# RMS norms of a hybrid decoder trunk: token sums on all partitions and the inverse root over the row

## Chip, cores, metric

The kernel runs on one NeuronCore of a Trainium2 chip. The metric is device time of one execution in microseconds (us). Engines are named as in the profile: PE (TensorE matmul), PEld (its weight loads), DVE (VectorE), ACT (ScalarE), POOL (GpSimd), SP (SyncE, which issues most DMAs).

## What is computed

A trunk of two layers over 1040 tokens (16 learned ones ahead of 1024) of 1024 features, in float32. There are five RMS norms over the features, and one more over groups of 256 features inside the Mamba-2 mixer:

```
def rmsnorm(x, w):
    y = x * lax.rsqrt(jnp.mean(x * x, axis=-1, keepdims=True) + 1e-5)
    return y * w
...
for layer in range(2):
    h = h + mixer[layer](rmsnorm(h, norm_mix[layer]))
    h = h + sq_relu_mlp(rmsnorm(h, norm_mlp[layer]), ...)
h = rmsnorm(h, norm_final)
# inside the mixer of layer 1, for each of 8 groups of 256 features
g = g * lax.rsqrt(jnp.mean(g * g, axis=-1, keepdims=True) + 1e-5)
```

The mixer of layer 0 is a linear recurrence beside a state-space model, that of layer 1 is Mamba-2 in chunks of 128 tokens ("SSD").

## The kernel before

**Layout.** The residual stream h lies in SBUF with features on the 128 partitions (eight slabs, index k) and tokens along the row. Tokens go in three tiles, `TT` = (0, 400), (400, 384), (784, 256), or without the 16 extra tokens `TL`, whose first tile is 384 wide. Weights and activations are split into a high and a low fp32r half, and each product is three matmuls (`mm3`, L182 to L184).

**A norm before.** It has two parts.
- `token_sums` (L246): the squares of the slabs are accumulated on ACT, POOL and DVE into one tile (`square`, L274; `sums` adds two accumulators at L287, and the last tile of the final norm hands over two). Then, for every 128 tokens, a matmul takes the 128 tokens of the accumulator as weights and a single column of ones as the moving operand (L253): the sums land with tokens on partitions, one column per 128 tokens. DVE scales them and adds epsilon (L258), and `rsqrt` (L187) takes the inverse root of this [128, 2 to 4] tile by an integer first guess (L193, L194) and three Newton steps of three operations each (L196 to L198).
- `token_bcast` (L266): for every 128 tokens a matmul with the root, repeated over 128 columns, as weights and the identity as the moving operand spreads it over all partitions (L270). The row then lies in PSUM and is read from there.

With fp32 operands each such product is two instructions in the trace.

**Who uses it.** 39 norms in all.
- `raw_stats` (L1019) for the first norm; the row is copied to SBUF by ACT (L1025), and the projections multiply by it when they leave PSUM.
- `factors` (L310) where the norm is applied late: `up_unit` copies the row to SBUF (L373) and multiplies at L375; `late2` (L1248) copies it for the last tile of the Mamba-2 mixer.
- `norm` and `apply` (L316, L290), for the first two tiles ahead of the Mamba-2 mixer: L296 multiplies, ACT and DVE or POOL split the result at L298 and L300.
- `final` (L324): the last norm, its multiplications at L338 (POOL, from a copy that ACT makes at L334) and L340 (DVE), and the output DMAs.
- `ssd_norm` (L1435): 8 groups by 3 tiles. L1457 multiplies, L1469 and L1470 split into yh and yl, and the output projection (`ssd_wout`, L1475) takes these as operands.

**Order of the work.** The two parts are steps of Python generators: between them other work is put out (`tick`, L133; `step`, L1542), in the SSD stretch some 18 us of PE work. The builder orders each engine's instructions by priority, which is the order in which they were written, moved by the offsets in `SHIFT` (L64) for `token_sums` and `token_bcast` among others. Each engine then runs its own list in order. PSUM has four buffers for product tiles (`mm`) and four small ones (`sm`), but two `mm` and three wide ones while the MLPs run. The sums and the row of a norm share one `sm` buffer.

**Other lines named below.** L176 and L177 split a weight tile (ACT cast, DVE or POOL difference). L1281, L1286 and L1287 take the SSD projections out of PSUM, through the short convolution and a tanh; L1302 and L1303 do so for the gates. L1390 and L1391 make the decay matrix of a chunk on ACT from a row that a DMA brings, POOL multiplies it (L1392), and L1406 uses it on PE. L1485 adds a projected tile to h. L599 and L607 add the MLP's result to h and scale it for the final norm. L922 and L923 are gate products of the layer 0 recurrence and their sigmoids, L927 an exponential, L1225 an exponential of the SSD time steps, L806 a transposition.

Of the kernel before, what the change touches and what calls it, by code (L numbers as in the profile page):

```python
# [18 lines left out]
P = 128  # L19
# [59 lines left out]
class Trunk:  # L79
    def __init__(self, ctx, tc, A, out, dbg=None):  # L80
        self.ctx, self.tc, self.nc, self.A, self.out = ctx, tc, tc.nc, A, out
        self.dbg = dbg or {}
        nc = self.nc
        self.cp = ctx.enter_context(tc.tile_pool(name="cp", bufs=1))
        self.wp = ctx.enter_context(tc.tile_pool(name="wp", bufs=2))
        self.tp = ctx.enter_context(tc.tile_pool(name="tp", bufs=2))
        self.sp = ctx.enter_context(tc.tile_pool(name="sp", reuse_waits="tile", bufs=2))
        self.pstack = None
        self.npsum = 0
        self.psum(False)  # L90
        ctx.callback(lambda: self.pstack.close())
        self.dr = ctx.enter_context(tc.tile_pool(name="dr", bufs=1, space=DRAM))
        cp = self.cp
        self.H = cp.tile([P, KT, NTOK], F32, name="h")
        self.h = [self.H[:, :, o:o + w] for o, w in TT]
        self.HI, self.LO = (cp.tile([P, KT, NTOK], F32R, name=q) for q in ("hi", "lo"))
        self.hi, self.lo = ([q[:, :, o:o + w] for o, w in TT] for q in (self.HI, self.LO))
        self.cols = cp.tile([P, NCOLS], F32, name="cols")
        nc.scalar.dma_start(self.cols, A["cols"])

        self.ident2 = cp.tile([P, 240], F32, name="ident")
        nc.gpsimd.memset(self.ident2[:, P:], 0.0)
        self.ident = self.ident2[:, :P]
        make_identity(nc, self.ident)
        self.ones = cp.tile([P, 1], F32, name="ones")
        nc.gpsimd.memset(self.ones, 1.0)

        nc.scalar.copy(self.cp.tile([P, 1], F32, name="first"), self.ones)

        pt = self.sm()  # L110
        for _ in range(5):
            nc.tensor.matmul(pt[:, :240], lhsT=self.ident, rhs=self.ident2, start=True, stop=True)
        self.later = deque()
        self.stage = "a"
        self.acc, self.rbs = {}, {}
# [68 lines left out]
        nc.tensor.matmul(pt, lhsT=wlo, rhs=xhi, start=False, stop=last)  # L184


    def rsqrt(self, s, n, tag="rs", m=P):  # L187

        nc, tp = self.nc, self.tp
        y = tp.tile([P, n], F32, name=tag + "y")  # L190
        t = tp.tile([P, n], F32, name=tag + "t")
        yi = y.bitcast(I32)
        nc.vector.tensor_scalar(out=yi[:m], in0=s[:m].bitcast(I32), scalar1=1, scalar2=None, op0=ALU.logical_shift_right)  # L193
        nc.vector.tensor_scalar(out=yi[:m], in0=yi[:m], scalar1=-1, scalar2=0x5F3759DF, op0=ALU.mult, op1=ALU.add)  # L194
        for _ in range(3):
            nc.vector.scalar_tensor_tensor(out=t[:m], in0=y[:m], scalar=-0.5, in1=y[:m], op0=ALU.mult, op1=ALU.mult)  # L196
            nc.vector.tensor_tensor(out=t[:m], in0=t[:m], in1=s[:m], op=ALU.mult)
            nc.vector.scalar_tensor_tensor(out=y[:m], in0=t[:m], scalar=1.5, in1=y[:m], op0=ALU.add, op1=ALU.mult)  # L198
        return y

    def exp_acc(self, out, x, shape, pool, tag):

        nc = self.nc
# [39 lines left out]
        v.scalar_tensor_tensor(out=out, in0=x, scalar=0.0, in1=e, op0=ALU.max, op1=ALU.add)  # L243

    @shifted
    def token_sums(self, accs, w, nfeat, st):  # L246

        nc, tp = self.nc, self.tp
        ch = [(o, min(P, w - o)) for o in range(0, w, P)]
        n = len(ch)  # L250
        for i, (o, l) in enumerate(ch):
            for j, a in enumerate(accs):
                nc.tensor.matmul(st[:l, 508 + i:509 + i], lhsT=a[:, o:o + l], rhs=self.ones, start=j == 0, stop=j == len(accs) - 1)  # L253
        s = tp.tile([P, 4], F32, name="ts_s")
        l = ch[-1][1]
        f = n if l == P else n - 1
        kw = dict(scalar1=1.0 / nfeat, scalar2=EPS, op0=ALU.mult, op1=ALU.add)
        nc.vector.tensor_scalar(out=s[:, :f], in0=st[:, 508:508 + f], **kw)  # L258
        if f < n:
            nc.vector.memset(s[:, f:n], 1.0)  # L260
            nc.vector.tensor_scalar(out=s[:l, f:n], in0=st[:l, 508 + f:508 + n], **kw)
        y = self.rsqrt(s[:, :n], n)
        return st, y, ch

    @shifted
    def token_bcast(self, sums, w):  # L266

        st, y, ch = sums
        for i, (o, l) in enumerate(ch):
            self.nc.tensor.matmul(st[:, o:o + l], lhsT=y[:l, i:i + 1].broadcast_to([l, P]), rhs=self.ident[:l, :l], start=True, stop=True)  # L270
        return st[:, :w]


    def square(self, i, k, off, w, pool=False, end=False):  # L274
# [7 lines left out]
            nc.scalar.activation(out=sq, in_=self.h[i][:, k, off:off + w], func=AF.Square)  # L282
            (nc.gpsimd if pool or k % 2 == 0 and not end else nc.vector).tensor_tensor(out=a, in0=a, in1=sq, op=ALU.add)

    def sums(self, i, w):
        a, b, *rest = [self.acc.pop((i, k)) for k in (0, 1, KT - 1) if (i, k) in self.acc]
        self.nc.vector.tensor_tensor(out=a, in0=a, in1=b, op=ALU.add)  # L287
        return self.token_sums([a] + rest, w, 1024, self.sm())

    def apply(self, wname, i, off, w, rb):  # L290

# [32 lines left out]
    def final(self, i):  # L324

        nc = self.nc
        o, w = TL[i]
        off = o - TT[i][0]
        st = self.sums(i, w)
        yield  # L330
        rb = self.token_bcast(st, w)
        if i < 2:
            rc = self.scr("s1", w)
            nc.scalar.copy(rc, rb)  # L334
        for k in range(KT):
            hs = self.h[i][:, k, off:off + w]
            if i < 2 and k % 2:
                nc.gpsimd.tensor_tensor(out=hs, in0=hs, in1=rc, op=ALU.mult)  # L338
            else:
                nc.vector.tensor_tensor(out=hs, in0=hs, in1=rb, op=ALU.mult)  # L340
            if k % 2:
                nc.sync.dma_start(self.out[k - 1:k + 1, :, o - META:o - META + w].rearrange("k p n -> p k n"),
                                  self.h[i][:, k - 1:k + 1, off:off + w])
# [674 lines left out]
    @shifted  # L1018
    def raw_stats(self, i):  # L1019

        o, w = TT[i]
        for k in range(KT):
            self.square(i, k, 0, w)
        st = self.sums(i, w)
        self.nc.scalar.copy(self.rb[:, o:o + w], self.token_bcast(st, w))  # L1025

    def split_y(self, i):

# [406 lines left out]
    def ssd_norm(self, pg, g, i):  # L1435

        nc = self.nc
        v = nc.vector
        o, w = TL[i]
        y = self.prod[g, "z", i]  # L1440
        m = o - TT[i][0]
        acc, sq = (self.prod[g, k, i][:, m:m + w] for k in ("x0", "x1"))
        nc.scalar.activation(out=acc, in_=y[:, 0], func=AF.Square)
        nc.scalar.activation(out=sq, in_=y[:, 1], func=AF.Square)
        nc.gpsimd.tensor_tensor(out=acc, in0=acc, in1=sq, op=ALU.add)
        yield
        yield
        sums = self.token_sums([acc], w, 256, self.sm())
        yield
        if i == 0:  # L1450
            self.flush()
            self.wo[g] = [self.load_w(self.A["ssd_out"][2 * g + j], pg, "o", lo_pool=(j == 1)) for j in range(2)]
        wo = self.wo[g]
        yield
        rb = self.token_bcast(sums, w)
        for j in range(2):
            v.scalar_tensor_tensor(out=y[:, j], in0=y[:, j], scalar=self.col("gnorm", 2 * g + j), in1=rb, op0=ALU.mult, op1=ALU.mult)  # L1457
        if g == 7 and i != 1:

            pool, q, wt = ((self.px, "xbc0", 400), None, (pg, "xbc1", 384))[i]  # L1460
            yh, yl = ([pool.tile([P, wt], F32R, name=q, bufs=6) for _ in range(2)] for _ in range(2))
            for j in range(2):
                nc.scalar.copy(yh[j][:, :w], y[:, j])
                v.tensor_tensor(out=yl[j][:, :w], in0=y[:, j], in1=yh[j][:, :w].bitcast(F32), op=ALU.subtract)
        else:
            self.flush(8)
            yh = pg.tile([P, 2, 384], F32R, name="yh", bufs=2)
            yl = pg.tile([P, 2, 384], F32R, name="yl", bufs=2)
            nc.scalar.copy(yh[:, :, :w], y)  # L1469
            v.tensor_tensor(out=yl[:, :, :w], in0=y, in1=yh[:, :, :w].bitcast(F32), op=ALU.subtract)  # L1470
            yh, yl = ([q[:, j] for j in range(2)] for q in (yh, yl))
        yield
        self.wq += [(g, wo, (yh, yl), i, n) for n in range(KT)]
# [132 lines left out]
    def run(self, stages="abcd"):  # L1606
        tc = self.tc
        if "a" not in stages:
            for i in range(3):
                self.load_h(i)  # L1610
        else:
            self.stage = "a"
            self.mixer0()
        if "a" in stages or "b" in stages:
            with tc.tile_pool(name="mlp0", reuse_waits="tile", bufs=2) as mp:
                self.pcw = 1040
# [109 lines left out]
```

## Time and profile before

| | us |
|---|---|
| median of 3 runs | 2750.51 (2750.38 to 2751.53) |
| profiled execution | 2749.45 |
| its span, first to last instruction | 2747.70 |
| PE busy | 2660.3 (97%) |
| DVE busy | 1954.4 (71%) |
| ACT busy | 1072.5 (39%) |
| POOL busy | 1017.0 (37%) |

The profile is of one execution. Busy time of PE is the union of matmuls whose ends are modelled, and matmuls overlap, so what an instruction takes of PE's queue is read from start to start. The stages in order: mixer of layer 0 to about 365 us, MLP 0 to about 1090, the SSD mixer to about 2050, MLP 1 and the final norm to the end.

### The profile page before, as it was taken

Reading aid. Unit: us, or ns where it says so; the run is one execution under the profiler, and the core shown is the slowest. Engines: PE = TensorE matmul, PEld = TensorE weight load, DVE = VectorE, ACT = ScalarE, POOL = GpSimd, SP = SyncE. Lnnn points to the kernel's source line nnn. Section 1 sums busy time; section 2 is a strip of 40 time slices with the busy share of each in tenths; the row PEclk is TensorE's granted clock in tenths of the full one; section 3 lists DMA queues with packets and bytes.
Section 4 is the critical chain, followed back from the end, with each engine's and each line's share of the span. In section 5 each row is a group of like instructions: output and inputs, shape, how many; then the busy total and the mean of one; then the engine's idle time right before and its main releaser. Section 6 shows DMA issues by size and latency. Waiting matters only on the chain.

```text
span 2747.7 us, 44368 instructions
## 1 busy us (share of the span) xinstructions
PE 2660.3 (97%) x17121; PEld 2545.9 (93%) x17121; DVE 1954.4 (71%) x3821; ACT 1072.5 (39%) x2162; POOL 1017.0 (37%) x826
## 2 busy tenths in 40 slices
PE   7888999999999999999999999999989999999998
PEld 7877999999999999899999999998988999999998
DVE  9977465666666686876867768677786666666685
ACT  5555343323332334443433434334454332333334
POOL 3101115444444432142332323323444554554542
PEclk9999999999999999999999999999999999999999
DMA  4432411111111110121221212213311111111111
GB/s 163 123 74 59 140 47 55 39 55 50 44 58 43 47 47 26 52 81 60 75 62 52 80 56 76 62 52 100 107 52 66 55 50 51 54 51 50 47 43 62
DMA packets 117907, 176.33 MB, mean 64 GB/s; under 512 B 13376, under 2 KB 47936, under 8 KB 117568
## 3 DMA queue, kind: packets, MB, share of 16 engines
q1 hardware_dynamic: 117408, 173.34, 20.2%
q8 instruction: 135, 2.21, 0.3%
q14 instruction: 76, 0.62, 0.1%
q10 hardware_dynamic: 288, 0.15, 0.0%
HBM read 158.34 MB, written 8.72 MB: 61 GB/s over the span
## 4 chain that ended last, share of the span: by engine, by line
PE 51%; DVE 6%; POOL 1%; ACT 1%; issue 1%; DMA 0%; SPq 0%; DVEq 0%; ACTq 0%; POOLq 0%
PE mm L182 12%; PE mm L183 12%; PE mm L184 12%; PE pd L182 3%; PE pd L184 3%; PE pd L183 3%; DVE xbc L1286 1%; PE sm L1410 1%; PE mm L1406 1%; PE mm L1403 1%; PE sm L1372 1%; PE sm L253 1%; PE sm L270 0%; DVE xbc L1288 0%; PE sm L1386 0%
## 5 line engine op out<-in xcount | busy, mean ns | idle before, releaser
L182 PE MATMUL mm<-hi,whi 128*128 128x384 f32 (+4 forms) x3120 | 1017.3, 326 | 10.4 <-ACT whi L176 8.6
L183 PE MATMUL mm<-lo,whi 128*128 128x384 f32 (+4 forms) x3120 | 1005.9, 322 | 0.9 <-DVE lo L300 0.5
L184 PE MATMUL mm<-hi,wlo 128*128 128x384 f32 (+4 forms) x3120 | 1003.0, 322 | 2.7 <-POOL wlo L177 2.7
L182 PEld LDWEIGHTS mm<-hi,whi 128*128 128x128 f32 x3120 | 589.7, 189 | 20.4 <-ACT whi L176 9.4
L183 PEld LDWEIGHTS mm<-lo,whi 128*128 128x128 f32 x3120 | 589.7, 189 | 7.2 <-DVE lo L300 0.8
L184 PEld LDWEIGHTS mm<-hi,wlo 128*128 128x128 f32 x3120 | 591.5, 190 | 3.7 <-POOL wlo L177 3.5
L182 PE MATMUL pd<-pc 128*128 128x260 f32 (+1 forms) x1176 | 377.1, 321 | 6.2 <-DVE s L375 2.2
L184 PE MATMUL pd<-pc 128*128 128x260 f32 (+1 forms) x1176 | 374.9, 319 | 0.0
L183 PE MATMUL pd<-pc 128*128 128x260 f32 (+1 forms) x1176 | 373.8, 318 | 0.0
L492 DVE TENSOR_TENSOR h<-h,pd 128x520 f32<-128x520 f32 (+1 forms) x336 | 291.9, 871 | 59.5 <-PE pd L184 45.2
L375 DVE SCALAR_TENSOR_TENSOR s<-mm,rb 128x384 f32<-128x384 f32 (+2 forms) x192 | 98.7, 515 | 266.6 <-PE mm L184 252.4
L389 POOL TENSOR_TENSOR pc<-ca,pc 128x512 fp32r<-128x512 f32 x112 | 169.4, 1513 | 244.9 <-ACT pc L388 164.3
L389 POOL TENSOR_TENSOR pc<-draw,pc 128x512 fp32r<-128x512 f32 x84 | 125.4, 1492 | 336.2 <-ACT pc L388 336.2
L182 PEld LDWEIGHTS pd<-pc 128*128 128x128 f32 x1176 | 221.7, 189 | 22.0 <-DVE acc L492 4.4
L184 PEld LDWEIGHTS pd<-pc 128*128 128x128 f32 x1176 | 221.8, 189 | 15.9
L183 PEld LDWEIGHTS pd<-pc 128*128 128x128 f32 x1176 | 221.9, 189 | 12.5
L176 ACT CAST whi<-wraw 128x512 fp32r<-128x512 f32 x286 | 167.8, 616 | 164.5 <-PE mm L183 144.0
L376 ACT ACTIVATE sq<-s 128x384 f32<-128x384 f32 (+2 forms) x192 | 94.1, 491 | 346.6 <-DVE s L375 346.5
L492 DVE TENSOR_TENSOR acc<-acc,pd 128x520 f32<-128x520 f32 (+1 forms) x234 | 190.4, 862 | 4.3 <-PE pd L184 4.1
L177 DVE TENSOR_TENSOR wlo<-wraw,whi 128x512 fp32r<-128x512 f32 x224 | 167.7, 767 | 19.9 <-ACT whi L176 11.5
L1392 POOL TENSOR_TENSOR csb<-csb,sc 128x512 f32<-128x512 f32 x64 | 89.7, 1401 | 211.2 <-DVE sc L1388 200.1
L388 ACT CAST pc<-cb 128x520 fp32r<-128x520 f32 (+1 forms) x112 | 70.0, 625 | 247.7 <-PE pd L184 130.8
(388 smaller groups left out, 4478.0 us busy)
## 6 DMA issues: line engine op xcount, KB each, us to landing
wraw<-in_mlp_up SPq DMA_DIRECT2D x128, 256.0 KB
wraw<-in_ssd_in SPq DMA_DIRECT2D x120, 256.0 KB
draw<-in_mlp_down SPq DMA_DIRECT2D x112, 256.0 KB
csb<-csd SPq DMA_DIRECT2D x64, 256.0 KB
ecb<-ecd SPq DMA_DIRECT2D x128, 64.0 KB
wraw<-in_ssd_out SPq DMA_DIRECT2D x32, 256.0 KB
wraw<-in_ev_in SPq DMA_DIRECT2D x24, 256.0 KB
wraw<-in_ev_out SPq DMA_DIRECT2D x18, 256.0 KB
```

Source lines behind the costliest of these rows:

```text
L176: nc.scalar.copy(h, raw)
L177: e.tensor_tensor(out=l, in0=raw, in1=h.bitcast(F32), op=ALU.subtract)
L182: nc.tensor.matmul(pt, lhsT=whi, rhs=xhi, start=first, stop=False)
L183: nc.tensor.matmul(pt, lhsT=whi, rhs=xlo, start=False, stop=False)
L184: nc.tensor.matmul(pt, lhsT=wlo, rhs=xhi, start=False, stop=last)
L253: nc.tensor.matmul(st[:l, 508 + i:509 + i], lhsT=a[:, o:o + l], rhs=self.ones, start=j == 0, stop=j == len(accs) - 1)
L375: nc.vector.scalar_tensor_tensor(out=r, in0=pt[:, :w], scalar=0.0, in1=rbs[i], op0=ALU.max, op1=ALU.mult)
L376: nc.scalar.activation(out=dst[:, o - t0:o - t0 + w].bitcast(F32), in_=r, func=AF.Square)
L388: nc.scalar.copy(hi, x)
L389: e.tensor_tensor(out=lo, in0=x, in1=hi.bitcast(F32), op=ALU.subtract)
L492: v.tensor_tensor(out=d, in0=d, in1=src, op=ALU.add)
L1392: nc.gpsimd.tensor_tensor(out=csb, in0=csb, in1=sc.unsqueeze(1).broadcast_to([P, 4, P]), op=ALU.mult)
```

## The change

All norms are computed in another form.
- `token_sums`: one matmul per accumulator with a full 128x128 matrix of ones as weights and the row of w accumulated squares as the moving operand. The sums land in PSUM already on all partitions. ACT then takes the logarithm (scaled by 1/n, with epsilon as bias, read from PSUM) and from it the exponential of minus one half of it: a first value of the inverse root, over the whole row, in SBUF.
- `token_bcast`: no matmul. Three DVE operations over the row make one Newton step, the second of them reading the sums in PSUM.
- `rsqrt` goes. The row now lies in SBUF: in `self.rb`, in a tile of a new pool `nr`, or in the accumulators of `ssd_norm`. The ACT copies in `raw_stats` and `final` go; those in `up_unit` and `late2` stay.

```diff
+        self.eps = cp.tile([P, 1], F32, name="eps")
+        nc.gpsimd.memset(self.eps, EPS)
...
-    def rsqrt(self, s, n, tag="rs", m=P):
...
     @shifted
-    def token_sums(self, accs, w, nfeat, st):
...
+    def token_sums(self, accs, w, nfeat, st, y):
+
+        nc = self.nc
+        for j, a in enumerate(accs):
+            nc.tensor.matmul(st[:, :w], lhsT=self.ones.broadcast_to([P, P]), rhs=a[:, :w], start=j == 0, stop=j == len(accs) - 1)
+        nc.scalar.activation(out=y, in_=st[:, :w], func=AF.Ln, scale=1.0 / nfeat, bias=self.eps)
+        nc.scalar.activation(out=y, in_=y, func=AF.Exp, scale=-0.5)
+        return st, y, nfeat
 
     @shifted
-    def token_bcast(self, sums, w):
...
+    def token_bcast(self, sums, w, t=None):
+
+        st, y, nfeat = sums
+        v = self.nc.vector
+        if t is None:
+            t = self.nr.tile([P, TW], F32, name="nrt")[:, :w]
+        v.scalar_tensor_tensor(out=t, in0=y, scalar=-0.5 / nfeat, in1=y, op0=ALU.mult, op1=ALU.mult)
+        v.scalar_tensor_tensor(out=t, in0=st[:, :w], scalar=nfeat * EPS, in1=t, op0=ALU.add, op1=ALU.mult)
+        v.scalar_tensor_tensor(out=y, in0=t, scalar=1.5, in1=y, op0=ALU.add, op1=ALU.mult)
+        return y
...
-    def sums(self, i, w):
+    def sums(self, i, w, y=None):
...
+        if y is None:
+            y = self.nr.tile([P, TT[i][1]], F32, name=f"nrm{i}")[:, :w]
+        return self.token_sums([a] + rest, w, 1024, self.sm(), y)
...
         rb = self.token_bcast(st, w)
-        if i < 2:
-            rc = self.scr("s1", w)
-            nc.scalar.copy(rc, rb)
...
-                nc.gpsimd.tensor_tensor(out=hs, in0=hs, in1=rc, op=ALU.mult)
+                nc.gpsimd.tensor_tensor(out=hs, in0=hs, in1=rb, op=ALU.mult)
...
-        st = self.sums(i, w)
-        self.nc.scalar.copy(self.rb[:, o:o + w], self.token_bcast(st, w))
+        self.token_bcast(self.sums(i, w, self.rb[:, o:o + w]), w, self.scr("s1", w))
...
-        sums = self.token_sums([acc], w, 256, self.sm())
+        sums = self.token_sums([acc], w, 256, self.sm(), sq)
...
-        rb = self.token_bcast(sums, w)
+        rb = self.token_bcast(sums, w, acc)
...
+        self.nr = self.ctx.enter_context(tc.tile_pool(name="nr", bufs=1))
```

## Rows read from the trace of the kernel before

**Rows 1.** The page: busy time of engines, and the chain that ended last.

```profile
PE 2660.3 (97%) x17121; PEld 2545.9 (93%) x17121; DVE 1954.4 (71%) x3821; ACT 1072.5 (39%) x2162; POOL 1017.0 (37%) x826
...
PE 51%; DVE 6%; POOL 1%; ACT 1%; issue 1%; DMA 0%; SPq 0%; DVEq 0%; ACTq 0%; POOLq 0%
```

**Rows 2.** Stretches: length, busy us of PE, PEld, DVE, ACT, POOL; clock, DMA.

```profile
1160.00:1860.00 700.00, 696.21 (x4670) 669.42 (x4669) 502.99 (x1226) 287.85 (x675) 224.23 (x213) 1.00 0.22 67
1860.00:2090.00 230.00, 212.16 (x1355) 199.33 (x1354) 183.86 (x434) 114.25 (x251) 100.56 (x90) 0.96 0.27 86
```

**Rows 3.** Whole span: busy PE and PEld of L253; L270's group by line.

```profile
0.00:2748.00 2748.00, 28.51 (x218) 30.55 (x218) 0.99 0.21 64
...
L270 PE MATMUL sm<-ident,rsy 128*128 128x128 f32 (+1 forms) x214 | 32.7, 283 | 11.1 <-DVE rsy L198 11.0
```

**Rows 4.** Timeline of PE, two places in the SSD stretch: start, length, instruction.

```profile
1349.85 0.72 PE L253 MATMUL sm<-ones,xbc 128*128 128x1 f32 x6
1350.43 0.37 PE L182 MATMUL mm<-hi,whi 128*128 128x260 f32 x1
...
1368.20 0.83 PE L270 MATMUL sm<-ident,rsy 128*128 128x128 f32 x6
1368.87 0.49 PE L1372 MATMUL sm<-ident,xbc 128*16 128x128 f32 x3
```

**Rows 5.** Timeline of PE, fp32 products of mixer 0.

```profile
106.83 2.69 PE L922 MATMUL mm<-h,gates 128*128 128x400 f32 x8 [0.76 <-DVE h L901]
109.35 0.27 PE L806 MATMUL sm<-ident,s5E 128*128 128x128 f32 x1
```

**Rows 6.** Waits of PE (us, times, longest); PE's timeline ahead of the SSD stretch.

```profile
PE sm L270 <- DVE rsy L198: 11.0, 9, 2.4
...
1094.21 0.93 PE L270 MATMUL sm<-ident,rsy 128*128 128x128 f32 x6 [1.05 <-DVE rsy L198]
1106.02 0.45 PE L182 MATMUL mm<-hi,whi 128*128 128x388 f32 x1 [0.57 <-ACT hi L298]
```

**Rows 7.** ACT: two groups by line and form; two places of its timeline.

```profile
L923 ACT ACTIVATE l_tr<-mm,cols 128x384 f32<-128x384 f32 x4 | 2.3, 577 | 0.7 <-PE mm L922 0.7
L282 ACT ACTIVATE s<-h 128x384 f32<-128x384 f32 x42 | 21.6, 518 | 25.8 <-DVE h L599 14.3 <-DVE rst L196 5.1 <-DVE h L1485 3.8
...
106.77 1.28 ACT L923 ACT_TABLE_LOAD   x1
108.06 1.43 ACT L923 ACTIVATE l_tr<-mm,cols 128x400 f32<-128x400 f32 x3
...
1147.41 1.28 ACT L1225 ACT_TABLE_LOAD   x1
1151.22 0.41 ACT L1225 ACTIVATE dec<-sm 128x288 f32<-128x288 f32 x1 [2.53 <-PE sm L1221]
```

**Rows 8.** ACT's longest wait, 1160 to 1860 us; timeline of ACT, then POOL.

```profile
ACT csb L1390 <- DMA csb<-csd: 127.1, 32, 8.2
...
1389.60 0.63 ACT L1391 ACTIVATE csb<-csb 128x512 f32<-128x512 f32 x1
...
1397.42 1.69 POOL L1392 TENSOR_TENSOR csb<-csb,sc 128x512 f32<-128x512 f32 x1 [9.56 <-DVE sc L1388]
```

**Rows 9.** DVE groups by line: a Newton line, and a row operation by form.

```profile
L197 DVE TENSOR_TENSOR rst<-rst,ts_s 128x3 f32<-128x3 f32 (+2 forms) x117 | 29.2, 250 | 2.0
...
L1288 DVE SCALAR_TENSOR_TENSOR xbc<-s,xbc 128x384 f32<-128x384 f32 x32 | 19.8, 619 | 0.3 <-ACT s L1287 0.3
```

**Rows 10.** Waits of PE for the split half yl (us, times, longest).

```profile
PE mm L183 <- DVE yl L1470: 1.6, 6, 0.4
```

**Rows 11.** The end of the kernel: timelines of ACT, PE and DVE.

```profile
2736.95 0.51 ACT L607 ACTIVATE h<-h,cols 128x256 f32<-128x256 f32 x1
...
2740.32 1.10 PE L270 MATMUL sm<-ident,rsy 128*128 128x128 f32 x4 [2.42 <-DVE rsy L198]
...
2741.46 2.74 DVE L340 TENSOR_TENSOR h<-h,sm 128x256 f32<-128x256 f32 x8 [1.19 <-PE sm L270]
```

More of the change, by code (lines that the diff above doesn't have):

```diff
@@ L184, in mm3 @@
         nc.tensor.matmul(pt, lhsT=wlo, rhs=xhi, start=False, stop=last)
-    def rsqrt(self, s, n, tag="rs", m=P):
[L189 to L199, printed above, removed]
     def exp_acc(self, out, x, shape, pool, tag):
@@ L245, in token_sums @@
     @shifted
-    def token_sums(self, accs, w, nfeat, st):
[L248 to L263, printed above, removed]
-    @shifted
-    def token_bcast(self, sums, w):
[L268 to L271, printed above, removed]
+    def token_sums(self, accs, w, nfeat, st, y):
[5 more added lines that the diff above has]
+        return st, y, nfeat
+    @shifted
+    def token_bcast(self, sums, w, t=None):
[7 more added lines that the diff above has]
+        return y
     def square(self, i, k, off, w, pool=False, end=False):
@@ L283, in square @@
             (nc.gpsimd if pool or k % 2 == 0 and not end else nc.vector).tensor_tensor(out=a, in0=a, in1=sq, op=ALU.add)
-    def sums(self, i, w):
+    def sums(self, i, w, y=None):
         a, b, *rest = [self.acc.pop((i, k)) for k in (0, 1, KT - 1) if (i, k) in self.acc]
         self.nc.vector.tensor_tensor(out=a, in0=a, in1=b, op=ALU.add)
-        return self.token_sums([a] + rest, w, 1024, self.sm())
+        if y is None:
+            y = self.nr.tile([P, TT[i][1]], F32, name=f"nrm{i}")[:, :w]
+        return self.token_sums([a] + rest, w, 1024, self.sm(), y)
     def apply(self, wname, i, off, w, rb):
```

## Prediction

> **What bounds the kernel now.** I began with the page: PE is busy for 97% of the span, and the chain that ended last lies on PE for just over half of it [rows 1]. The view by stretches shows how even this is: while the eight SSD groups run, PE is busy for 696 of 700 us at full granted clock, ACT for 288 and DVE for 503; only in the last group and the change of layers, 1860 to 2090 us, is PE free for 18 of 230 us [rows 2]. PE takes its work in order, so time taken off its queue shortens the run wherever nothing else is late; a stall costs in full.
>
> The norms' own share came next. The column sums (L253) are 218 instructions and the spreading of the root (L270) 214 [rows 3]. Their mean durations of 131 ns (28.51 by 218) and 283 ns aren't comparable prices, since matmuls overlap. The timeline gives what they hold of the queue: six sums from 1349.85 to the next matmul at 1350.43, 0.097 us each; six spreads from 1368.20 to 1368.87, 0.112 us each [rows 4].
>
> **PE's part of the change.** Removed: 218 x 0.097 = 21.1 us and 214 x 0.112 = 24.0 us, together 45.1. Added: one fp32 product per accumulator, 128 ones columns against w token columns. The nearest row is L922, also fp32 with 128x128 weights, two instructions per product: its first eight are, by the loop's order, products of 400, 384, 256 and 400 columns, and PE took 2.52 us from 106.83 to the next line's work at 109.35 [rows 5], so 1.75 ns per column. The widths in TT and TL give 3 x 1040 columns for the first three norms, 8 x 1024 for the SSD norms, 1024 for the second MLP's, and 1024 plus a second 256 for the final one (its last tile hands over two accumulators): 13,616 columns, 23.8 us. Net: **-21.3 us**, 16 x 0.58 + 8 x 0.38 = 12 us of it inside the SSD stretch (w = 384: 6 x 0.209 - 0.67; w = 256: 4 x 0.209 - 0.45). The uncertainty of the two issue prices is some 3 us.
>
> **PE's waits for the root.** PE now stands still nine times for the last Newton step, 11.0 us in all [rows 6]. L270 leaves PE, so these stops go; what is late next is the consumer. At 1094.21 a stop of 1.05 us goes, but the same norm's split pieces then stop PE at 1106.02 in any case [rows 6], and PE will arrive there earlier. One stop of 2.42 us belongs to the tail, counted below. Of the other 8.6 us I take half, **-4**; bounds 0 and -8.6.
>
> **ACT's part.** Ln isn't in this trace. Bounds for it: the PSUM-reading activation with a bias column, 577 ns at 384 columns, and the plain SBUF one, 518 ns, which I also take for Exp [rows 7]. A table load is 1.28 us [rows 7]. The trace has no Ln next to an Exp, so a norm may bring no load, one or two; I take two, since sigmoid and Exp, too, bring one each way. A norm then puts 0.58 + 0.52 + 2 x 1.28 = 3.66 us on ACT, 39 norms 143 us, against five PSUM copies that go. Where it hides: in the SSD stretch ACT waits 127 us in 32 gaps for the decay DMA alone, and the decay it makes is early: finished from 1389.60 on, picked up by POOL at 1397.42, after 9.56 us of waiting for DVE [rows 8]. The load needn't wait for PE: at 1147.41 one ran, then its Exp waited another 2.53 us for the matmul [rows 7]. So I cost the 24 SSD norms at nothing; without that cover it is up to 3.66 us each. Behind Ln in ACT's queue stand the evacuations of PSUM (L1281, L1302), the weight casts (L176) and the squares; DVE's weight halves and PE wait for those. At the layer changes and in the end stretch, where squares and casts stand close to PE's need, I take **+2** for 15 norms; bounds -3 and +12.
>
> The Trainium skill (page ScalarE: Activation LUTs, section What ACT_TABLE_LOAD costs) prices a switch at about 2.66 us, a drain of 1.38 us behind the load. Here the row disagrees: load at 106.77 for 1.28 us, next activation at 108.06 [rows 7]. By the page ACT would hold 78 x 1.38 = 108 us more and the tail grow by another 2.8 us, by the rows neither.
>
> **DVE's part.** Each norm loses twelve tiny operations; L197's three are 250 ns each, so twelve like them are 3.0 us per norm, 117 us in all [rows 9]. It gains three over the full row, like L1288's at 619 ns for 384 columns [rows 9]: 1.86 us per norm, some 63 us in all with the narrower tiles. DVE is relieved. But the place moves: the old work was done soon after the sums, the new three stand with the spreading, right ahead of the multiplication that needs them. In the SSD stretch some 18 us lie between sums and spreading (1349.85 to 1368.20 [rows 4]), so Ln and Exp are hidden there. For the first token tile of each group the way on is tight already: PE waited six times for the split half yl, 1.6 us [rows 10]. If all 1.86 us come before it, six stops cost 11 us; if the three run in DVE's gaps before, nothing. I take **+4**. Queued behind them on DVE are the conv steps L1286 and the residual adds L1485, which free PE's mm buffers; at 28% free time (197 of 700 us [rows 2]) these catch up. The final norm loses its ACT copies and POOL then reads the row directly; the multiplications keep their sizes: nothing.
>
> **The tail.** The last norm lies open. Now: spread at 2740.32, first multiplication at 2741.46; ACT's last square-side work ends at 2736.95 + 0.51 = 2737.46 [rows 11]. After: load to 2738.74, Ln 0.58, load 1.28, Exp 0.52, three row operations 1.86: 2742.98. That is **+1.5** (384-column prices for 256, so rather less); with no load at all -0.6; with the squares pushed back by the tile before, +3.
>
> **Sum.** -21.3 - 4 + 2 + 4 + 1.5 = -17.8 us. The profiled execution took 2749.45 us (span 2747.70 and 1.75 around it), 1.1 below the median of 2750.51; applied to the median this is 2732.7, rounded to 2732. About 0.2%, 5.5 us, is what a measurement of this kernel can tell from no change.
>
> **Rivals.**
> - *ACT's queue becomes the wait (slower).* Place: Ln stands in ACT's queue for the sums while a PSUM tile behind it isn't emptied, and PE runs out of its four mm buffers. Price: if half of 3.66 us reaches PE in the 24 SSD norms, 24 x 1.83 = 44 us against 25 gained: +19, **2769**. It decides from 25 / 39 = 0.65 us of PE stop per norm. For it: ACT is in order and the loads are new to this stretch. Against: rows 8. Chance 0.13.
> - *DVE's late row operations eat it.* All six tight places at 11 us, no stop recovered (0 for -4): -21.3 + 11 + 2 + 1.5 = -7, **2744**. For it: rows 10; against: DVE's gaps. Chance 0.14, half of it within 5.5 us of now.
> - *One load for Ln and Exp.* If both sit in one table, the load between them goes: the tail loses 1.28 us and each layer change as much in latency, some -3, **2729**. Only loads in front of other functions are in the trace. Chance 0.12. The Trainium skill (same page, Table sets: the hidden batching unit) says that one set holds both and that ln then exp costs one load; no run here shows it.
> - *Shorter chains.* Twelve hops on a crowded DVE become two on ACT and three on DVE; at the layer changes the root then comes early, all 8.6 us are kept and DVE's relief pays: -21.3 - 8.6 - 2 = -32, **2718**. Chance 0.09.
>
> My forecast has 0.52.
>
> **How the numbers follow.** Faster: 0.52 + 0.12 + 0.09 + 0.07 = 0.80; the same 0.07; slower 0.13. The range goes from 2714 (shorter chains, with 3 us of price error) to 2752 (the late row operations with +8 more at the layer changes); it leaves out the ACT rival and little else.
>
> **What would show it.** Right: L270 gone; L253 at 80 instructions, some 24 us of queue; PE's instructions down by 352; up to 78 more loads; no new PE wait on ACT in the SSD stretch. Wrong: PE waits for mm tiles whose release hangs on L1281 or L176, yl waits of over 1 us per group, or a first multiplication in the tail later than 6 us after the sums' start. The forecast is wrong if PE's busy time falls by 20 us and the span doesn't follow.

## The result, and the profile after

The changed kernel is slower: 2764.91 us median of 4 runs (2763.73 to 2766.59) beside 2750.45 us for the kernel before on the same chip (2747.55 to 2751.53, 4 runs). That is +14.5 us where -18 was forecast: outside the range, and on the other side. The ratio of the runs is given as 1.0065, 95% interval 1.0052 to 1.0077, a little above the quotient of these two medians (1.0053); by either it is slower. Here the two ways differ by 3 us, below by up to 2. The profiled execution has a span of 2762.0 us against 2747.7.

The busy times on the page of the kernel after, answering [rows 1]:

```profile
PE 2645.5 (96%) x16769; PEld 2523.2 (91%) x16769; DVE 1951.4 (71%) x3464; ACT 1207.0 (44%) x2312; POOL 1025.6 (37%) x827
```

The view by stretches, answering [rows 2, 3]: the SSD groups, and L238, the ones product, alone over the whole span (columns as there).

```profile
1176.00:1876.00 700.00, 692.94 (x4589) 664.57 (x4590) 502.86 (x1081) 355.83 (x755) 232.27 (x217) 1.00 0.23 68
...
0.00:2762.00 2762.00, 33.64 (x80) 15.01 (x80) 0.98 0.21 64
```

PE got its relief: 352 instructions fewer, 14.8 us less busy time, 80 instructions of ones products. In the SSD groups ACT is busy for 356 of 700 us instead of 288, and PE still for 693. The span did not follow. The waits of PE after, answering [rows 6, 10] (us, times, longest):

```profile
PE sm L238 <- DVE sa L269: 26.2, 9, 5.1
...
PE mm L185 <- DVE yl L1450: 0.2, 1, 0.2
```

The same stop before, ahead of the column sums, which the prediction didn't look at:

```profile
PE sm L253 <- DVE sa L287: 8.6, 6, 3.8
```

The stops for the root (L270) are gone, and so are those for yl; but PE now stands 26.2 us for the accumulator that the sums need. What is late there is DVE, and DVE waits for ACT. The waits of DVE at its first row operation (L250), by tile, and the table loads on ACT after, answering [rows 7]:

```profile
DVE xbc L250 <- ACT xbc L240: 34.9, 13, 3.0
...
DVE nrt L250 <- ACT nrm L240: 26.7, 11, 4.8
...
DVE s L250 <- ACT rb L240: 4.1, 2, 2.3
```

```profile
L239 ACT ACT_TABLE_LOAD x39 | 50.0, 1283 | 35.6 <-PE sm L238 35.1
L240 ACT ACT_TABLE_LOAD x37 | 47.5, 1283 | 0.7
```

All norms but two bring two loads of 1.28 us, 76 in all, and DVE stands 26 times, 65.7 us together, at the head of its queue for Exp. In the SSD groups (xbc, 34.9 us) nothing comes of it. At the layer changes (nrt) the residual additions (L580) and the square sums (L265, L269), which PE waits for, stand behind.

To see where the time went I followed five instants, one same instruction each, in the timeline of PE: the first of MLP 0's last products (before: 1042.49), the first SSD state product (1162.62), the first down product of MLP 1 (2079.34), the first of its last products (2686.78) and the end of the span (2747.7). After, they are at:

```profile
1048.75 0.45 PE L184 MATMUL mm<-acc,pc 128*128 128x400 f32 x1 [0.52 <-DVE s L356]
...
1176.51 0.66 PE L1390 MATMUL sm<-xte,btok 16*128 16x256 f32 x2 [1.02 <-DVE xte L1359]
...
2085.71 0.77 PE L184 MATMUL pd<-pc 128*128 128x512 f32 x1 [4.43 <-DVE s L356]
...
2693.50 0.44 PE L184 MATMUL mm<-acc,pc 128*128 128x384 f32 x1 [0.52 <-DVE s L356]
```

Five stages follow, by subtraction; the table gives before in us and each kernel's difference to it, for one profiled execution each (labels are those of the experiments below). A profiled execution is not the median one: that of e3 took 3.5 us more than its median, those of e9 and e12 3.3 and 3.2 less.

| kernel | mixer 0, MLP 0 | change to mixer 1 | SSD to MLP 1 | MLP 1 | tail | span |
|---|---|---|---|---|---|---|
| before | 1042.5 | 120.1 | 916.7 | 607.4 | 60.9 | 2747.7 |
| after | +6.3 | +7.6 | -7.5 | +0.4 | +7.6 | +14.3 |
| e1 new in SSD alone | +1.5 | +1.5 | -10.7 | +2.1 | 0.0 | -5.6 |
| e2 new outside SSD | +5.4 | +6.7 | +0.6 | +1.6 | +7.4 | +21.6 |
| e3 no loads | +3.7 | +3.4 | -17.8 | +0.6 | +0.7 | -9.4 |
| e8 loads behind | +3.2 | +7.1 | -7.1 | -1.0 | +2.2 | +4.4 |
| e9 root in PSUM | +7.9 | +0.8 | -8.2 | -1.0 | +3.5 | +3.0 |
| e10 no loads, PSUM | +1.8 | -3.9 | -17.6 | +0.5 | -3.3 | -22.5 |
| e11 mixed | +2.8 | -4.4 | -12.2 | +1.5 | -3.1 | -15.3 |
| e12 mixed, group 7 | -3.1 | -4.6 | -12.5 | +1.2 | -3.1 | -22.1 |

The first stage must be read with care: e11 and e12 have the same work there, and their two executions differ by 5.9 us. The kernels whose norms wait for loads there (after, e2, e9, and e7 with +12.0) have +5.4 to +12.0, the others but e5 -3.1 to +3.7, so a part of the +6.3 may be the loads; that is not shown. The other stages repeat within some 3.5 us where the code is the same (MLP 1 is the same in all).

The table leaves out PE's granted clock, which has two levels: 2.4 GHz (1.00 in the views) and 1.2 GHz (0.50). First the change to mixer 1 before, after and in e11; then six us of it after; then PE's ones product of 256 columns there, after and in e11 (columns as in [rows 2] and [rows 4]).

```profile
1042.49:1162.62 120.13, 113.82 (x710) 108.72 (x710) 91.92 (x226) 48.08 (x100) 24.85 (x24) 1.00 0.10 29
1048.75:1176.51 127.76, 115.03 (x678) 109.95 (x679) 94.33 (x199) 57.24 (x110) 25.05 (x24) 0.95 0.09 28
1045.32:1161.05 115.73, 110.06 (x679) 105.82 (x679) 92.86 (x202) 47.68 (x101) 24.23 (x24) 1.00 0.10 31
...
1116.00:1122.00 6.00, 4.96 (x15) 4.78 (x16) 4.20 (x10) 4.04 (x6) 0.71 (x1) 0.50 0.14 44
...
1117.05 1.22 PE L238 MATMUL sm<-sa,ones 128*128 128x256 f32 x2 [4.04 <-DVE sa L269]
...
1104.72 0.70 PE L240 MATMUL sm<-sa,ones 128*128 128x256 f32 x2 [2.09 <-DVE sa L278]
```

In the kernel after PE stood still for 4.04 us and then had 0.50 of the clock; the same product took 1.22 us instead of 0.70. For one instruction fewer than e11 PE is busy 5 us longer in this stage (115.03 and 110.06). So a stop cost more here than its own length. At the end of the SSD stage PE is busy for 86.19 us after at a clock of 0.92 and 81.89 in e10 at 0.96, in the tail for 50.81 at 0.87 and 47.96 at 0.94, with the same instructions.

The tail after, answering [rows 11]: timelines of DVE and PE, POOL's multiplications beside them, and ACT's last square-side work.

```profile
2738.47 0.56 DVE L250 SCALAR_TENSOR_TENSOR nrt<-nrm 128x384 f32<-128x384 f32 x1 [2.37 <-ACT nrm L240]
...
2741.06 5.11 DVE L321 TENSOR_TENSOR h<-h,nrm 128x384 f32<-128x384 f32 x4
2746.09 0.41 DVE L265 TENSOR_TENSOR sa<-sa,s 128x256 f32<-128x256 f32 x1
2746.43 0.74 DVE L580 TENSOR_TENSOR h<-h,mm 128x256 f32<-128x256 f32 x2
...
2749.56 0.42 DVE L269 TENSOR_TENSOR sa<-sa 128x256 f32<-128x256 f32 x1
...
2755.76 2.77 DVE L321 TENSOR_TENSOR h<-h,nrm 128x256 f32<-128x256 f32 x8
```

```profile
2750.03 1.22 PE L238 MATMUL sm<-sa,ones 128*128 128x256 f32 x2 [5.09 <-DVE sa L269]
```

```profile
2740.89 4.87 POOL L319 TENSOR_TENSOR h<-h,nrm 128x384 f32<-128x384 f32 x4 [8.76 <-DVE nrm L252]
...
2750.13 0.51 ACT L588 ACTIVATE h<-h,cols 128x256 f32<-128x256 f32 x1
```

Two things delay PE's last sums here. The row operations wait for Exp. Then four multiplications by the root hold DVE for 5.11 us while POOL does the other four; the residual additions of the last tile stand behind them. Before, the same four took 1.95 us:

```profile
2730.22 1.95 DVE L340 TENSOR_TENSOR h<-h,sm 128x384 f32<-128x384 f32 x4
```

### The profile page after: what moved, and what is told of

It is laid out like the page before. It is cut to its first block, busy times and chain, and to the rows that moved or that the text cites. A ratio compares the mean times of both kernels' runs of the same rounds, so it can differ in the third digit from the quotient of the medians.

```text
span 2762.0 us, 43481 instructions
## 1 busy us (share of the span) xinstructions
PE 2645.5 (96%) x16769; PEld 2523.2 (91%) x16769; DVE 1951.4 (71%) x3464; ACT 1207.0 (44%) x2312; POOL 1025.6 (37%) x827
## 4 chain that ended last, share of the span: by engine, by line
PE 76%; DVE 8%; ACT 3%; issue 2%; POOL 1%; DMA 0%; SPq 0%; ACTq 0%; DVEq 0%; POOLq 0%
PE mm L184 17%; PE mm L185 17%; PE mm L186 17%; PE pd L184 6%; PE pd L185 6%; PE pd L186 6%; PE sm L1390 1%; DVE xbc L1266 1%; PE mm L1386 1%; PE mm L1383 1%; PE sm L1352 1%; PE sm L238 1%; DVE wlo L179 1%; DVE xbc L1268 1%; ACT hi L291 0%
## 5 line engine op out<-in xcount | busy, mean ns | idle before, releaser
L184 PEld LDWEIGHTS mm<-hi,whi 128*128 128x128 f32 x3120 | 590.3, 189 | 30.5 <-ACT whi L178 11.3
L185 PEld LDWEIGHTS pd<-pc 128*128 128x128 f32 x1176 | 221.6, 188 | 12.2
```

The costliest lines, as they stand in the source:

```text
L184: nc.tensor.matmul(pt, lhsT=whi, rhs=xhi, start=first, stop=False)
L185: nc.tensor.matmul(pt, lhsT=whi, rhs=xlo, start=False, stop=False)
```

## Experiments

Theory A: the saving of the SSD groups arrives, and the loss sits at the start, the layer changes and the tail. Its causes as I came to see them: A1, the loads; P, the multiplications that now read the root from SBUF.

**e1, e2: one half each.**

```
# e1: kernel before, with the new functions under other names
-        sums = self.token_sums([acc], w, 256, self.sm())        # in ssd_norm alone
+        sums = self.row_sums([acc], w, 256, self.sm(), sq)
# e2: kernel after, the old functions in ssd_norm alone
```

> The new form in the 24 norms inside the SSD groups alone, the form of before in the 15 others. Theory A (the loss of 24 us sits at the start, the changes of layer and the tail; the saved PE work of the SSD groups arrives): the kernel is faster than before, by 9 to 13 us, near 2739 us; the two table loads per SSD norm cost PE nothing, and the PE waits at the layer changes are those of before (stops for the column sums near 9 us). Rival B (each of the 39 norms costs the kernel about the same, some 0.4 us): slower than before, near 2759. Rival C (the 10 us that the SSD groups seemed to gain were only time that PE had lost ahead of them, caught up): no gain, near 2750.

Measured: 2740.83 us beside 2747.09, ratio 0.9973 (0.9962 to 0.9985), some 7 us faster.

> The reverse: the new form in the 15 norms outside the SSD groups, the form of before inside them (its three small scratch tiles share one buffer for room). Theory A: the loss without the gain, near 2774 us (+24). Rival B: +6, near 2756. Rival C: the loss is the whole difference of the two kernels, +14, near 2765.

Measured: 2767.25 us, ratio 1.0066 (1.0053 to 1.0079), 18 us slower by the ratio, 20 by the medians. The signs are those of theory A, the sizes smaller (7 where 9 to 13 were expected, 18 to 20 where 24); B falls by both, C by e1. The table puts e2's loss where the changed kernel has it, and e1's gain in the SSD stage: from the first SSD product to the first product of 260 columns after 1900 us it took 800.9 us (1165.63 to 1966.49) against 815.5 before (1162.62 to 1978.07).

**e3: no loads.**

```
-        nc.scalar.activation(out=y, in_=st[:, :w], func=AF.Ln, scale=1.0 / nfeat, bias=self.eps)
+        nc.scalar.activation(out=y, in_=st[:, :w], func=AF.Identity, scale=1.0 / nfeat, bias=self.eps)
```

> The changed kernel with Ln replaced by Identity (same operands, scale and bias; the values of the roots are therefore not those of the reference). Every instruction of the change stays, but Identity is in the table that Exp uses, so 74 of the 76 table loads go. Theory A1 (the two loads, 2.56 us in each norm's chain, make DVE's first row operation and with it PE late): DVE's waits at that operation fall from 66 us to under 20, PE's stops at the ones product from 26 us to under 10, and the time falls to 2738 to 2746 us, below the kernel before. Rival A2 (two more steps on ACT's in-order queue and three full-row operations late on DVE do it, loads or not): 2758 to 2765.

Measured: 2736.54 us beside 2747.09, ratio 0.9955 (0.9942 to 0.9968). A1 holds: two loads are left, and the waits are

```profile
PE sm L238 <- DVE sa L269: 16.7, 7, 4.0
...
DVE nrt L250 <- ACT nrm L240: 8.9, 6, 3.1
DVE xbc L250 <- ACT xbc L240: 4.6, 6, 0.8
```

DVE's waits fall from 65.7 to 13.5 us as expected; PE's stops fall less than expected, 26.2 to 16.7 (under 10 was expected). By spans the loads cost 23.7 us (+14.3 against -9.4), by the ratios some 30; of the 23.7 they cost 6.9 in the tail, 10.2 from SSD to MLP 1, 4.2 at the change to mixer 1. Those 10.2 lie at the end of that stage: the steady groups took 803.6 us after (1176.51 to 1980.15) and 803.2 here (1169.73 to 1972.93), so in them the loads cost nothing. The stops are not all of it: after that product PE is busy for 82.00 us here, with one instruction fewer, and 86.19 after, at a granted clock of 0.96 and 0.92.

**e4: one activation and no load.**

```
-  Ln(scale 1/nfeat, bias eps); Exp(scale -0.5)
+  nc.scalar.activation(out=y, in_=st[:, :w].bitcast(I32), func=AF.Exp,
+                       scale=-0.5 * math.log(2) / 2 ** 23, bias=self.seed[nfeat])
+  # four row operations: t = 64/9/n*y*y; t *= st + n*EPS; t = (t - 10/3)*t; y = (t + 5)*y
```

> The changed kernel with one ACT instruction per norm instead of two: Exp alone, on the sum's bits read as an integer (an integer is 2^23 times a rough logarithm), and a cubic correction of four row operations on DVE in place of the Newton step of three. It computes the reference. Theory A1: as without the loads, less one ACT step and plus one row operation of 0.56 us per norm, 2738 to 2746 us. Rival A2: one ACT instruction less but one DVE operation more per norm, so still 2755 to 2765.

Measured: 2743.49 us beside 2747.09, ratio 0.9984 (0.9976 to 0.9993): inside A1's numbers, so the loads and not the change as such. From SSD to MLP 1 it gained 9.6 us, e3 17.8; the fourth row operation may be what takes the rest, but no run tried it alone.

**e5, e8: the loads, but nobody waits for them.** In e5 a Ln and an Exp on a constant column stand behind each norm's Exp.

> The kernel without loads (Identity in Ln's place, so other values for the roots) with a Ln and an Exp on one column added behind each norm's Exp: ACT does the two table loads again, 2.56 us and two tiny activations per norm, but nothing waits for their results. Theory A1a (the loads cost because DVE's first row operation waits for Exp behind them): the time stays near that without loads, 2737 to 2744 us, and DVE's waits at that operation stay under 25 us. Rival A1b (the loads cost because they hold up the squares and casts behind them in ACT's queue): most of the 25 us between the changed kernel and the one without loads comes back, 2755 to 2765, with PE's stops at the ones product over 22 us.

Measured: 2829.32 us beside 2746.68, and the test missed its aim. The added operations depend on nothing, so the order that the builder plans put them at the start: from 60.35 us on ACT does one load after another, and the first stage took 96 us more. The later stages are those of e3 within 2 us (123.4, 897.0, 606.4, 61.7 us). e8 ties them to the norm:

```
         nc.scalar.activation(out=y, in_=y, func=AF.Exp, scale=-0.5)
+        nc.scalar.copy(self.dum[:, :1], y[:, :1])
+        nc.scalar.activation(out=self.dum[:, 1:2], in_=self.dum[:, :1], func=AF.Ln, bias=self.ones)
+        nc.scalar.activation(out=self.dum[:, :1], in_=self.dum[:, 1:2], func=AF.Exp)
```

> The kernel without loads (Identity in Ln's place, so other values for the roots), with three operations on one column added on ACT behind each norm's Exp and tied to its result: a copy, a Ln and an Exp. So both table loads (2.56 us) and some 0.6 us of tiny activations stand on ACT per norm again, in their place, but nothing outside ACT waits for them. The earlier try let them run at the start. Theory A1a (the loads cost because the root, and with it DVE's first row operation, comes later): 2737 to 2745 us; DVE's waits at that operation under 25 us; the tail as without loads, within 2 us of 61.6. Rival A1b (they cost because they hold up what stands behind them on ACT): 2755 to 2765, PE's stops at the ones product over 22 us, as in the changed kernel.

Measured: 2753.81 us beside 2748.01, ratio 1.0023 (1.0014 to 1.0032), between the two theories, and the waits show both:

```profile
PE sm L239 <- DVE sa L273: 25.4, 7, 5.4
...
DVE sa L269 <- ACT s L268: 14.5, 17, 1.8
DVE nrt L254 <- ACT nrm L241: 9.0, 7, 3.1
```

DVE no longer waits for the root (9.0 us), but for squares that stand behind the loads on ACT (14.5 us; 8.5 in e3, 8.1 in the kernel after), and PE's stops are back at 25.4. Of the loads' 23.7 us, 13.8 are back (+4.4 against -9.4). Of these, 3.4 stand in the steady groups (806.6 us against 803.2 in e3), where the loads of the kernel after cost nothing; they can be due to the three small operations, so through ACT's queue it is some 10 us. The stages say where: the change to mixer 1 is as in the kernel after (127.2 and 127.8 us), and from the product of 260 columns to MLP 1 7.2 of 9.8 us are back (103.0 here, 95.8 in e3, 105.6 after), so there the queue decides; the tail has only 1.5 of its 6.9 us back, so there it is the chain.

**e6: without the last group.** `... if g < 7 else` the form of before.

> The new form in the 21 norms of SSD groups 0 to 6 alone; group 7, whose norms stand among the squares of the next layer, and all others in the form of before. With the new form in all eight groups the stretch from the last group to MLP 1 was 3.9 us longer than before. Theory A (the new form costs wherever its chain isn't covered, the last group included): those 3.9 us come back at the price of one eighth of the saving, so 1 to 4 us faster than with all eight groups, 2737 to 2740, and 2747 minus 9 or so. Rival (the 3.9 us belong to how the eight groups end earlier, waiting for weights): nothing comes back, 2741 to 2743.

Measured: 2739.32 us beside 2746.68, ratio 0.9971 (0.9962 to 0.9981). The time lies in theory A's range, but the ratio is that of e1 (0.9973), and from the product of 260 columns to MLP 1 it took 104.8 us, e1 105.2 and the kernel before 101.3. Nothing came back, so the last group's norms were not what that stage lost: it is 3.5 us longer than before with the same code.

**e7: row operations one turn later.** `yield; yield` in place of one `yield` in the three norms outside SSD.

> The changed kernel with the three row operations (and what follows them) of the norms at the layer changes and at the end issued one turn later, behind one more residual unit, Ln and Exp with both loads where they were. Theory A1a (DVE stands at the head of its queue for Exp while residual additions and square sums that PE needs stand behind): DVE's waits at the first row operation fall by a third or more, the stretch from the end of MLP 0 to the first SSD product falls from 127.8 us to 121 to 125, and the time to 2752 to 2760. Rival (the chain's own length decides: the normalized pieces come late, wherever DVE stands): no gain or a loss, 2763 to 2772.

Measured: 2767.48 us, ratio 1.0074 (1.0056 to 1.0091). It tells little: the planned order moved, but DVE's waits at L250 at the layer changes stayed (27.9 us for nrt), so the edit did not remove what it was to remove; the change to mixer 1 was 1.8 us shorter, the first stage 5.7 longer, which its scatter can give.

**e9, e10: the root back in PSUM**, in the kernel after and in e3.

```
-        v.scalar_tensor_tensor(out=y, in0=t, scalar=1.5, in1=y, op0=ALU.add, op1=ALU.mult)
+        y0, y = y, st[:, :w] if psum else y
+        v.scalar_tensor_tensor(out=y, in0=t, scalar=1.5, in1=y0, op0=ALU.add, op1=ALU.mult)
# psum=True in norm and final; in final, as before the change, for i < 2:
+            nc.scalar.copy(rc, rb)                # and POOL multiplies by rc
```

> The changed kernel with one thing as before: for the second mixer's first two norms and the final norm the last row operation writes the root back to PSUM, DVE's multiplications read it there, and POOL reads a copy in SBUF that ACT makes. In the changed kernel DVE's eight final multiplications of 384 columns took 1322 ns each with the root in SBUF while POOL multiplied too; before they took 550 ns with the root in PSUM. Theory P (two SBUF inputs on DVE collide with POOL's reads, and these 2 x 4 multiplications hold the residual additions behind them): the eight go back to 550 to 600 ns, the tail falls from 68.5 us to 62 to 65, the change of layer by 1 to 2 us, the time to 2756 to 2761. Rival Q (they are slow because they start late, or cost nothing that the end waits for): the tail stays over 67 us, the time 2763 to 2766.

Measured: 2755.95 us beside 2748.01, ratio 1.0027 (1.0016 to 1.0037): theory P, though the change to mixer 1 gained more than the 1 to 2 us expected. The groups of DVE by form, first the kernel after, then e9:

```profile
L321 DVE TENSOR_TENSOR h<-h,nrm 128x384 f32<-128x384 f32 x8 | 10.1, 1322 | 0.0
...
L280 DVE SCALAR_TENSOR_TENSOR s<-h,cols,nrm 128x400 f32<-128x400 f32 x8 | 6.1, 803 | 0.9 <-POOL lo L284 0.9
...
L321 DVE TENSOR_TENSOR h<-h,nrm 128x256 f32<-128x256 f32 x8 | 2.8, 419 | 0.0
```

```profile
L281 DVE SCALAR_TENSOR_TENSOR s<-h,cols,sm 128x400 f32<-128x400 f32 x8 | 4.7, 627 | 0.6 <-POOL lo L285 0.6
...
L325 DVE TENSOR_TENSOR h<-h,sm 128x384 f32<-128x384 f32 x8 | 3.9, 550 | 0.3 <-ACT s L319 0.2
```

With the root in PSUM the eight take 550 ns again, beside the same work on POOL; the last tile's eight (256 columns), which have no POOL work beside them, took 419 ns with the root in SBUF all the same. So it is the place of the operand together with POOL. By spans it cost 11.3 us (+14.3 against +3.0), by the ratios some 10: 6.9 at the change to mixer 1, 4.1 in the tail. Inside the SSD groups the root lies in SBUF, too, and there the multiplications of 384 columns (L1437) took 644 ns against 607 before.

> Both taken away: no loads (Identity in Ln's place, so other values for the roots) and the root in PSUM for these norms. If loads and port are the two separate causes, the gains add: without loads was 10.6 us under the kernel before, the port gives 4 to 8 more, so 2728 to 2733 us beside 2747, near the saving that was forecast. If the port matters only while the chain is late from the loads, 2735 to 2738.

Measured: 2726.74 us beside 2748.01, ratio 0.9918 (0.9906 to 0.9930), 21 us faster, just below the range. The two causes add: 23.7 and 11.3 us alone, 36.8 together (+14.3 against -22.5); by the ratios 30, 10 and 40. Some 10 of the 36.8 us are longer busy time of PE for the same 16769 instructions, 2645.5 us after and 2635.9 here, at a granted clock of 0.983 and 0.988 over the span.

**e11, e12: versions that beat both kernels.** e11 takes Ln, Exp and one Newton step inside SSD, e4's form elsewhere, and the root in PSUM; e12 gives e4's form to group 7 too.

> A version that should beat both kernels and computes the reference: inside the SSD groups the change as it is (Ln, Exp, one Newton step), where its loads are covered; outside, Exp on the sum's bits and the cubic step, so no load there, and the root in PSUM as above. Theory: the SSD saving of 10 us, the start and MLP 0 about as before, the changes of layer and the tail 0 to 3 us better than before: 2733 to 2738 us. If the late row operations on DVE cost by themselves at the layer changes: 2739 to 2743, no better than the new form in the SSD groups alone.

Measured: 2733.91 us beside 2748.01, ratio 0.9946 (0.9934 to 0.9959), 14 us faster than before and 31 faster than the change.

> The mixed version with the last SSD group's three norms also by Exp on the sum's bits and the cubic step, so that no norm outside groups 0 to 6 brings a table load. In the changed kernel the stretch from the last group to MLP 1 lost 9.8 us against the version without loads, while the steady groups lost nothing. If that loss is the loads of group 7's norms, which stand among the squares of the next layer: the stretch from the first SSD product to MLP 1 falls from 904.5 us to 898 to 901 and the time by 3 to 6 us, to 2728 to 2731 beside a before of 2748. If it is the later norms' loads (those of MLP 1, gone already in the mixed version) or the cubic step's extra row operation takes it back: within 2 us of the mixed version, 2732 to 2736.

Measured: 2730.57 us beside 2749.53, ratio 0.9937 (0.9924 to 0.9951). The total is in the first theory's reach, but its reason fails: the stretch from SSD to MLP 1 is 904.2 us against 904.5, and what e12's profile has over e11's lies in the first stage, where the two do the same work. So taking group 7's loads away gained nothing in this form; whether they cost nothing, or the fourth row operation takes back what they cost, this run doesn't tell. Of the 10 us at the end of that stage, MLP 1's own norms account for about 5: from that product of 260 columns to MLP 1 it took 105.6 us after, 100.7 in e11. Why e3 needs only 95.8 there stays open in part: its chain is one row operation shorter, and that alone was not tried. 1.8 of the 4.9 us between the two are PE's busy time, 83.81 us in e11 at a granted clock of 0.93 and 82.00 in e3 at 0.96, with the same instructions.

## Why the prediction was wrong

**PE's part was right.** Instructions fell by 352. The 12 us inside the SSD stretch came: 815.5 us before, 803.6 after, 803.2 without loads. PE's busy time fell by 14.8 us, not 20, and by 24.4 in e10 (2635.9 us) with the same instructions: the price of PE's work holds, and some 10 us of it went to the lower clock in the stages with stops. The prediction's "a stall costs in full" was too little: it cost more.

**PE's waits for the root (-4) and DVE's late row operations (+4)** cancelled in the sum and neither came as put. L270's stops went, and yl's waits went from 1.6 to 0.2 us instead of growing. The stops moved to the sums: 8.6 to 26.2 us. Nor was DVE relieved by 117 less 63 us: its busy time went from 1954.4 to 1951.4.

**The step that failed first is ACT's part**, "I take +2 for 15 norms; bounds -3 and +12". I priced what two loads do to ACT's queue, and let nothing wait for the root at the head of DVE's. The loads cost 23.7 us by spans, twice the upper bound: e8 shows some 10 through the squares and casts behind them on ACT; the rest, by e8's waits and tail, goes through the root that comes later. The prediction's own sentence on it (squares and casts "stand close to PE's need") named the place and underpriced it. For the norms of the steady SSD groups, "at nothing" was right; for the last group it is not told apart.

The reason given, "the load needn't wait for PE", holds in some norms only. Rows of ACT after, in one SSD group: in the first norm the load ran ahead and Ln waited, in the second the load itself began after the sums. The last row is from the view of line L239: six times the line has a semaphore instruction on ACT's queue, and their first and last start, 1284.7 and 1848.4, are those of the six loads that came late.

```profile
1359.92 1.28 ACT L239 ACT_TABLE_LOAD   x1
1362.90 0.58 ACT L239 ACTIVATE xbc<-sm,eps 128x384 f32<-128x384 f32 x1 [1.70 <-PE sm L238]
...
1397.51 1.28 ACT L239 ACT_TABLE_LOAD   x1 [5.84 <-PE sm L238]
...
L239 ACTq EVENT_SEMAPHORE  x6: 17/17/17, 1284.7 to 1848.4; - x6
```

**The second is half a sentence**: "the multiplications keep their sizes: nothing". They keep their sizes and not their durations, 550 to 1322 ns, since the root moved from PSUM to SBUF. That was 11.3 us by spans, more than any term of the sum but PE's, and it could have been asked of [rows 11], which names the PSUM operand. The Trainium skill (page SBUF — State Buffer, section Who interferes with whom) states that a DVE instruction with two SBUF inputs contends with a GpSimd instruction that reads SBUF; these rows agree.

**The tail** was put at +1.5 and took +7.6: without loads +0.7, with the root in PSUM as well -3.3. What the term priced came nearly as put: from the end of ACT's last square-side work to the first multiplication it is 5.1 us after (2750.64 to 2755.76) and 4.0 before (2737.46 to 2741.46), +1.1. The other 6.5 us came before the last sums, where the tile ahead held DVE; the term took their start as unchanged and kept +3 for squares pushed back.

**The rivals.** The one on the slower side gave 2769, close to the 2764.9 measured, and is no more right than the forecast: its place was the SSD stretch and PE's buffers, and there nothing was lost. One load for the pair did not come (39 and 37 loads); the Trainium skill's sentence for it (page ScalarE: Activation LUTs, section Table sets: the hidden batching unit) says that ln then exp is one load, and that does not hold for this program. Shorter chains, -32 us, went too far: without its two costs the change is worth 21 us (e10). That is close to the forecast's 18, so two costs were missing; but as the two terms of 4 cancelled, the closeness is in part luck.

## What to carry to other kernels

Where a function moves to another engine, follow its result to the engine that consumes it: what stands behind the consumer in that queue pays for the producer's latency, table loads included, and only a stretch with slack in that queue hides it. Where PE stands still for it, look at the granted clock behind the stop as well. When an operand moves from PSUM to SBUF, look at what the other vector engine does at that moment before calling the instruction unchanged. And a change that is good in one stage and bad in another is best split: here the half alone, and then a form without loads and with the root in PSUM for the other half, gave some 7 and 18 us.

## What the runs showed of the hardware

- A DVE multiplication of 128x384 fp32 takes 1322 ns with both inputs in SBUF while POOL multiplies from SBUF, 550 ns with one input in PSUM beside the same POOL work. POOL's own go from 1076 to 1249 ns.
- Ln followed by Exp is two table loads in nearly every norm (39 and 37 loads for 39 norms), 1283 ns each, with the next activation right behind (load at 2752.64, Exp at 2753.93).
- A table load does not always run ahead of its activation's wait: six loads of the SSD groups began only after the sums, 5.84 us after ACT fell idle, and the line has six semaphore instructions on ACT's queue.
- After a stop of PE of 4.04 us the granted clock was 0.50, and a ones product of 256 columns took 1.22 us in place of 0.70 in e11.
- One order of instructions scatters by several us in the first stage (1045.3 and 1039.4 us to the same product in e11 and e12), so a difference of that size there says nothing in one execution.
